# Two blocks with expert layers on one core: where the background work stands in the queues of VectorE and GpSimd

## Chip, cores and metric

The kernel runs on 1 core of one Trainium2 chip. The metric is the device time of one execution in microseconds (us), the median over several runs.

## What is computed

256 tokens (batch 1) of width 2048 pass through two blocks, all in fp32. A block is a mixer and then an expert layer, each added to its input:

```python
x = x + mixer(rmsnorm(x, g_mix))        # first block: latent attention and sparse attention, gated
x = x + peer_ffn(rmsnorm(x, g_ffn), w_q, sub_keys, u_emb, v_emb)
x = rmsnorm(x, g_final)                 # second block: the same with mLSTM and an S5 recurrence as mixer
```

The expert layer chooses, per token and for each of 8 heads, 16 of 16,384 experts, and the recurrence's matrices come from a few parameters:

```python
def peer_ffn(x):                          # 128 tokens at a time
    q = einsum('td,dhk->thk', x, w_q)     # 8 heads, each in two halves of 64
    s = einsum('thpc,hpnc->thpn', q, sub_keys)
    s1, i1 = top_k(s[:, :, 0], 16);  s2, i2 = top_k(s[:, :, 1], 16)
    top_s, pos = top_k(s1[..., :, None] + s2[..., None, :], 16)
    expert = (i1 * 128 + i2) at pos;  g = softmax(top_s)
    a = gelu(einsum('thkd,td->thk', u_emb[expert], x))
    return einsum('thk,thkd->td', g * a, v_emb[expert])

def s5(u):                                # 64 states for each of 64 groups
    dt = exp(log_dt);  a = exp(lam * dt)              # complex
    b = ((a - 1) / lam) * B
    state = scan(state * a + b @ u);  y = Re(C @ state) + d * u
```

## The kernel before

**Products.** All matrix products run over all experts: no weight is gathered. An fp32 operand is split in a high part and the rest (`w_hi` and `w_lo`, `hT_hi` and `hT_lo`), and each product is three matmuls, hi by hi, hi by lo, lo by hi, in `products` (L214; the matmul is L220). `weights_now` (L196) brings one weight tile of 128 x 2048 in two halves: DMAs on SyncE (L203), the cast to `w_hi` on ScalarE (L205), and the subtraction that makes `w_lo` on VectorE (L211) or, for the last `pool` columns, on GpSimd (L209). `w_raw`, `w_hi` and `w_lo` have four half buffers each, so two tiles can be in the making or in use.

**The expert layer** is `peer` (L328), called twice. After the query products and the top-k of the keys, two rounds `r` follow; each takes 64 of the 128 first keys:

- product U: 64 weight tiles, two for one `ps_u`; `hT` is the operand of all. For the first 28 tiles of round 0 GpSimd makes 768 of 2048 columns of `w_lo` (`UP`, `UN`).
- beside it the gates, a dense matrix of each token's weight for each expert: 32 groups of 8 tokens. `prepare` (L487) makes one-hot matrices of the chosen indices, `oh1` on GpSimd (L491; 6 of 8 tokens in round 0, `G0`, all in round 1, the rest on VectorE), then `oh2`, `rh` and `rl` on VectorE (L494, L498, L499). `use` multiplies them on TensorE into `ps_g` (L505, L506).
- product V: 64 weight tiles, with the coefficients (`coef_hi`, `coef_lo`, L259, L260) as the other operand. Its stationary operand starts on a multiple of 64 bytes of a partition.

In round 0 the gates need `routing` (L406) for the two blocks of 128 tokens: a top-k over candidates on VectorE and a choice by one-hot (`oh`, the multiply L462 on GpSimd, 128 x 2048).

**Background work.** Gates, routing and other side work are generators in the list `K.bg`. After each weight tile the foreground calls `K.step(n)` (L151), which runs their next pieces until a credit of `n` us is used up. A scheduler then sorts each engine's instructions, by its own model of the times, so what was emitted first need not stand first. `behind(ins)` (L188) adds a condition of order: what is emitted inside it stands on `ins`'s engine after `ins`. Before, background pieces have none.

**The preparation of the recurrence** is one such piece, `_s5_prepare` (L1094), for the second mixer; nothing needs it before. It is handed to the first expert layer as `later` and begins when the 32 groups of gates of round 0 are emitted, within product U (`st["groups"] == T // TG`, L539). It makes on VectorE long chains of small operations on `s_prm` (L1066 to L1163) and `s_work`; 16 tables of three operations on GpSimd (L1194, L1195, L1196), which go out by DMA (L1201, L1202 for the decay, copied on VectorE before); and eight times an expansion of 2 x 6 operations (L1212 to L1221), one on VectorE and one on GpSimd, with transposes and small products on TensorE between them. The first expansion reuses the tables' buffer.

**Addresses.** `hT` (L284) is two tiles of 16,384 bytes a partition in a pool at the top, above 448 bytes of padding (`pad3`). They start at 196,128 and 212,512 of a partition, 32 bytes past a multiple of 64. The same tiles hold the operands of the two output projections (`mh`, `ml` in `mix1`, `ch`, `cl` in `mix2`). `o_hi` and `o_lo` of the first mixer start on multiples of 64 (124,928 for the first).

**Names of stretches.** Cut where the first weight DMA of each product is issued: U1a 664 to 1152 us, V1a 1152 to 1528, U1b 1528 to 1904, V1b 1904 to 2252 in the first expert layer (a is round 0, b round 1); U2a 2790 to 3197, V2a to 3546, U2b to 3922, V2b to the end in the second.

Of the kernel before, what the change touches and what calls it, by code (L numbers as in the profile page):

```python
# [9 lines left out]
OP = mybir.AluOpType  # L10
AX = mybir.AxisListType

P = 128
T = 256
TB = 2
D = 2048
KD = D // P
# [16 lines left out]
class Ctx:  # L34


    def __init__(self, ctx, tc):
        self.tc, self.nc = tc, tc.nc
        nc = self.nc
# [4 lines left out]
        self.wp = pool("weights", 2)  # L44
        self.pad = pool("pad", 1)
        self.two = pool("pairs", 2)
        self.pad3 = pool("pad3", 1, side="right")
        self.top = pool("hT", 1, side="right")
        for p, n in ((self.pad, 0), (self.pad3, 448)):
            if n:  # L50
                nc.gpsimd.memset(p.tile([P, n // 4], F32, name="pad"), 0.0)
        self.ps = pool("psum", 2, space=bass.MemoryType.PSUM)
# [18 lines left out]
        self.fine = 0  # L71
        self.last = None

    def defer(self, fn):
# [76 lines left out]
    def step(self, n):  # L151


        self.credit = min(self.credit, 0.0) + n
        idle = 0
        while self.credit > 0 and idle < len(self.bg):
            lane = self.bg.pop(0)
            try:
                took = next(lane)
            except StopIteration:  # L160
                continue
            self.bg.append(lane)
            self.credit -= took
            idle = 0 if took else idle + 1

    def lane(self):
# [29 lines left out]
    def weights_now(self, src, n, pool):  # L196
        nc = self.nc
        self.fine -= 1
        h = n // 2
        raw, hi, lo = ([self.wp.tile([P, D // 2], d, name=nm, bufs=4)[:, :h] for _ in range(2)]  # L200
                       for nm, d in (("w_raw", F32), ("w_hi", F32R), ("w_lo", F32R)))
        for i in range(2):
            nc.sync.dma_start(raw[i], src[:, i * h:(i + 1) * h])  # L203
        for i in range(2):
            nc.scalar.copy(hi[i], raw[i])  # L205
        for i in range(2):
            m = max(0, min(h, (2 - i) * h - pool))
            if m < h:
                nc.gpsimd.tensor_tensor(lo[i][:, m:], raw[i][:, m:], hi[i][:, m:].bitcast(F32), op=OP.subtract)  # L209
            if m:  # L210
                nc.vector.tensor_tensor(lo[i][:, :m], raw[i][:, :m], hi[i][:, :m].bitcast(F32), op=OP.subtract)  # L211
        return Halves(hi, h), Halves(lo, h)
# [70 lines left out]

    def hT(self):  # L284
        return (self.top.tile([P, KD, T], F32R, name="hT_hi"),
                self.top.tile([P, KD, T], F32R, name="hT_lo"))

# [40 lines left out]
def peer(K, wq, keys, u, v, g_out, g_next=None, dst=None, later=None):  # L328
# [156 lines left out]
    def gates(r, on_pool):  # L485

        def prepare(t0):  # L487
            oh1 = K.two.tile([P, TG, P], F16, name="oh1", tag="two_a", bufs=2)
            for t in range(TG):
                e = nc.gpsimd if t < on_pool else nc.vector  # L490
                e.tensor_scalar(oh1[:, t], K.iota, i1T[:, t0 + t:t0 + t + 1], None, op0=OP.is_equal)  # L491
            oh2 = rp.tile([P, TG, NJ], F16, name="oh2", bufs=2)
# [42 lines left out]
    for r in range(2):  # L535
        st.update(done=0, groups=0, A=[rp.tile([P, 16, T], F32, name="acts", tag="acts", bufs=4) for _ in range(4)])
        K.bg.append(gates(r, 8 if r else G0))
        for jp in range(NJ // 2):
            if r == 0 and st["groups"] == T // TG and later is not None:  # L539
                K.bg.append(later(rp))  # L540
                later = None
            ps = K.ps.tile([P, 2, T], F32, name="ps_u", bufs=2)
# [17 lines left out]
        if later is not None:  # L560
            K.bg.append(later(rp))
            later = None
# [120 lines left out]
def mix1(K, I):  # L683
# [7 lines left out]
    ps_v = lambda shape: K.ps.tile(shape, F32, name="ps_v", bufs=4)  # L691

    grow = b8([P, D], "gain_row")[0:1]
    nc.sync.dma_start(grow, I["norm_mix_row"])
# [300 lines left out]
    for i in range(KD):  # L995
# [9 lines left out]
        nc.vector.tensor_tensor(m, m, g1, op=OP.add)  # L1005
    mh, ml = K.hT()
    for q in range(4):
# [268 lines left out]
def mix2(K, I, dram):  # L1276
# [332 lines left out]
    for h in range(MH):  # L1609
# [4 lines left out]
        ready["h"] = h + 1  # L1614
    ch, cl = K.hT()

# [180 lines left out]
```

## Time and profile before

| | |
|---|---|
| median of 3 runs | 4299.8 us (4299.35 to 4306.35) |
| the profiled execution, time | 4299.48 us |
| its span on the core | 4297.4 us |
| mean granted clock of TensorE | 0.981 |
| PE, DVE, ACT, POOL busy | 97%, 66%, 47%, 36% |

PE is TensorE's matmuls, PEld its weight loads, DVE VectorE, ACT ScalarE, POOL GpSimd, SP SyncE. A table by stretches has in each row the stretch in us and its length, then for each engine its busy time and, behind an x, its instructions, then the granted clock of TensorE (1.00 is 2.4 GHz, 0.50 is 1.2 GHz), the DMA engines' busy share and GB/s. A row of waits names the engine, tile and line that waited, what it waited for, and then us in total, times, and the longest in us. A group of instructions has line, engine, operation, out<-in with shapes, the count, and then busy us and the mean of one in ns. A timeline row has start and length in us, the instruction, how many in a row, and in brackets the idle time before it and what ended that.

### The profile page before, as it was taken

Reading aid. Unit: us, or ns where it says so; the run is one execution under the profiler, and the core shown is the slowest. Engines: PE = TensorE matmul, PEld = TensorE weight load, DVE = VectorE, ACT = ScalarE, POOL = GpSimd, SP = SyncE. Lnnn points to the kernel's source line nnn. Section 1 sums busy time; section 2 is a strip of 40 time slices with the busy share of each in tenths; the row PEclk is TensorE's granted clock in tenths of the full one; section 3 lists DMA queues with packets and bytes.
Section 4 is the critical chain, followed back from the end, with each engine's and each line's share of the span. In section 5 each row is a group of like instructions: output and inputs, shape, how many; then the busy total and the mean of one; then the engine's idle time right before and its main releaser. Section 6 shows DMA issues by size and latency. Waiting matters only on the chain. (4 is left out here: it accounts for less than half of the span.)

```text
span 4297.4 us, 74404 instructions
## 1 busy us (share of the span) xinstructions
PE 4149.5 (97%) x29233; PEld 3827.3 (89%) x29233; DVE 2831.5 (66%) x4666; ACT 2019.8 (47%) x2848; POOL 1535.1 (36%) x1318
## 2 busy tenths in 40 slices
PE   8999999888999999999998999999999999999999
PEld 7999989778888899998888998999998889999887
DVE  6775559887557656665556556798855556665565
ACT  5565443433344444445553455444445554444554
POOL 1100023789214147730005452369910006772000
PEclk9999999999999999999998999999999999999999
DMA  5445554454456655555666555545555555555555
GB/s 178 162 150 189 182 175 141 145 169 144 154 201 218 208 184 180 178 181 193 201 207 207 177 164 176 165 143 177 171 179 192 195 195 181 180 180 185 192 204 167
DMA packets 234160, 769.95 MB, mean 179 GB/s; under 512 B 44304, under 2 KB 46352, under 8 KB 233041
## 3 DMA queue, kind: packets, MB, share of 16 engines
q1 hardware_dynamic: 227906, 742.96, 52.5%
q0 software_dynamic: 5904, 22.25, 1.4%
q8 instruction: 229, 3.75, 0.3%
q14 instruction: 121, 0.99, 0.1%
HBM read 748.85 MB, written 16.25 MB: 178 GB/s over the span
## 5 line engine op out<-in xcount | busy, mean ns | idle before, releaser
L211 DVE TENSOR_TENSOR w_lo<-w_raw,w_hi 128x1024 fp32r<-128x1024 f32 (+3 forms) x1347 | 1631.8, 1244 | 1220.9 <-issue 941.6
L205 ACT CAST w_hi<-w_raw 128x1024 fp32r<-128x1024 f32 (+1 forms) x1388 | 1445.5, 1045 | 1603.9 <-PE ps_v L220 632.7
L220 PE MATMUL ps_u<-hT_hi,w_hi 128*128 128x256 f32 x5712 | 1404.0, 287 | 15.4 <-ACT acts L555 7.1
L220 PE MATMUL ps_u<-hT_lo,w_hi 128*128 128x256 f32 x5712 | 1387.1, 284 | 0.0
L491 POOL TENSOR_SCALAR oh<-iota_h,i1T 128x128 f16<-128x128 f16 x896 | 910.1, 1033 | 659.8 <-PE ps_v L220 492.7
L220 PEld LDWEIGHTS ps_u<-hT_hi,w_hi 128*128 128x128 f32 x5712 | 1098.6, 192 | 18.2 <-ACT acts L555 7.6
L220 PEld LDWEIGHTS ps_u<-hT_lo,w_hi 128*128 128x128 f32 x5712 | 1098.8, 192 | 1.9
L220 PE MATMUL ps_u<-hT_hi,w_lo 128*128 128x256 f32 x5712 | 739.2, 281 | 32.0 <-POOL w_lo L209 21.2
L220 PEld LDWEIGHTS ps_u<-hT_hi,w_lo 128*128 128x128 f32 x5712 | 699.8, 189 | 36.2 <-POOL w_lo L209 22.2
L220 PE MATMUL ps_v<-w_hi,coef_lo 128*128 128x512 f32 x2048 | 692.8, 390 | 2.4 <-DVE coef_lo L260 2.3
L220 PE MATMUL ps_v<-w_hi,coef_hi 128*128 128x512 f32 x2048 | 689.5, 390 | 0.0
L220 PE MATMUL ps_v<-w_lo,coef_hi 128*128 128x512 f32 x2048 | 512.5, 389 | 0.0
L220 PEld LDWEIGHTS ps_v<-w_hi,coef_lo 128*128 128x128 f32 x2048 | 383.1, 188 | 83.2 <-DVE coef_lo L260 4.4
L220 PEld LDWEIGHTS ps_v<-w_hi,coef_hi 128*128 128x128 f32 x2048 | 384.5, 188 | 79.7
L220 PEld LDWEIGHTS ps_v<-w_lo,coef_hi 128*128 128x128 f32 x2048 | 384.3, 188 | 79.6
L209 POOL TENSOR_TENSOR w_lo<-w_raw,w_hi 128x768 fp32r<-128x768 f32 (+3 forms) x159 | 310.1, 1957 | 353.3 <-PE ps_u L220 154.5
L259 ACT CAST coef_hi<-acts 128x512 fp32r<-128x512 f32 x256 | 159.4, 624 | 181.1 <-PE ps_v L220 177.8
L260 DVE TENSOR_TENSOR coef_lo<-acts,coef_hi 128x512 fp32r<-128x512 f32 x256 | 184.3, 721 | 6.0 <-ACT coef_hi L259 6.0
L119 POOL TENSOR_TENSOR normed<-x,gain 128x512 f32<-128x512 f32 x22 | 37.1, 1708 | 367.5 <-DVE x L96 280.1
L505 PE MATMUL ps_g<-rh,oh 128*128 128x64 f16 x1024 | 85.5, 197 | 40.8 <-POOL oh L491 35.5
L498 DVE TENSOR_TENSOR rh<-oh,g_hi 128x512 f16<-128x512 f16 x128 | 102.4, 800 | 19.8 <-PE ps_g L506 19.8
L515 ACT ACTIVATE acts<-ps_g 128x128 f32<-128x128 f32 (+7 forms) x318 | 60.6, 255 | 113.9 <-DVE acts L512 113.7
(490 smaller groups left out, 3573.2 us busy)
## 6 DMA issues: line engine op xcount, KB each, us to landing
w_raw<-in_p_u SPq DMA_DIRECT2D x512, 512.0 KB, 4.1
w_raw<-in_p_v SPq DMA_DIRECT2D x512, 512.0 KB, 4.3
w_raw<-in_in_gates SPq DMA_DIRECT2D x64, 512.0 KB, 4.0
w_raw<-in_w_out SPq DMA_DIRECT2D x64, 512.0 KB, 3.8
w_raw<-in_p_q SPq DMA_DIRECT2D x48, 512.0 KB, 4.1
w_raw<-in_in_t SPq DMA_DIRECT2D x38, 512.0 KB, 4.1
w_raw<-in_w_ab SPq DMA_DIRECT2D x32, 512.0 KB, 4.0
w_raw<-in_in_qk SPq DMA_DIRECT2D x32, 512.0 KB, 3.7
```

Of the source, the lines that this page charges most:

```text
L119: eng.tensor_tensor(self.normed_cols(tb, c), self.x[:, tb, cc], gb[:, cc], op=OP.mult)
L205: nc.scalar.copy(hi[i], raw[i])
L209: nc.gpsimd.tensor_tensor(lo[i][:, m:], raw[i][:, m:], hi[i][:, m:].bitcast(F32), op=OP.subtract)
L211: nc.vector.tensor_tensor(lo[i][:, :m], raw[i][:, :m], hi[i][:, :m].bitcast(F32), op=OP.subtract)
L220: self.last_mm = self.nc.tensor.matmul(out, lhsT=a, rhs=b, start=start, stop=stop)
L259: self.nc.scalar.copy(hi, src)
L260: return self.nc.vector.tensor_tensor(lo, src, hi.bitcast(F32), op=OP.subtract)
L491: e.tensor_scalar(oh1[:, t], K.iota, i1T[:, t0 + t:t0 + t + 1], None, op0=OP.is_equal)
L498: nc.vector.tensor_tensor(rh, oh2, b2(gh), op=OP.mult)
L505: nc.tensor.matmul(ps[:, t], lhsT=oh1[:, t], rhs=rh[:, t], start=True, stop=False)
L515: nc.scalar.activation(dst(nd, 16), src(nd, 16), AF.Copy, scale=1.0 / GS)
```

## The change

It keeps in `K.lo` the `w_lo` subtraction that was emitted last on VectorE and on GpSimd, and on GpSimd the last one-hot too. `step` runs each piece of background inside `behind` of both, so a piece can no longer stand on these two engines ahead of them. `later` is no longer started within product U, but after it, wrapped in `pin`, which puts the same condition on each of its pieces wherever they are run from. `hT` becomes one tile with 32 spare bytes: with the standard shift it starts where it did; with shift 0, for the operands of the two output projections, it starts at 196,096 and 212,480. The first mixer makes an 8-column tile first, so that its other tiles lie 32 bytes further up (`o_hi` at 124,960).

```diff
@@ Ctx.__init__ @@
-        self.pad = pool("pad", 1)
...
-        for p, n in ((self.pad, 0), (self.pad3, 448)):
-            if n:
-                nc.gpsimd.memset(p.tile([P, n // 4], F32, name="pad"), 0.0)
+        nc.gpsimd.memset(self.pad3.tile([P, 112], F32, name="pad"), 0.0)
...
+        self.lo = [None, None]
@@ step @@
-                took = next(lane)
+                with self.behind(self.lo[0]), self.behind(self.lo[1]):
+                    took = next(lane)
...
+    def pin(self, lane):
+
+        while True:
+            with self.behind(self.lo[0]), self.behind(self.lo[1]):
+                took = next(lane, None)
+            if took is None:
+                return
+            yield took
@@ weights_now @@
-                nc.gpsimd.tensor_tensor(lo[i][:, m:], raw[i][:, m:], hi[i][:, m:].bitcast(F32), op=OP.subtract)
+                self.lo[1] = nc.gpsimd.tensor_tensor(lo[i][:, m:], raw[i][:, m:], hi[i][:, m:].bitcast(F32), op=OP.subtract)
             if m:
-                nc.vector.tensor_tensor(lo[i][:, :m], raw[i][:, :m], hi[i][:, :m].bitcast(F32), op=OP.subtract)
+                self.lo[0] = nc.vector.tensor_tensor(lo[i][:, :m], raw[i][:, :m], hi[i][:, :m].bitcast(F32), op=OP.subtract)
@@ hT @@
-        return (self.top.tile([P, KD, T], F32R, name="hT_hi"),
-                self.top.tile([P, KD, T], F32R, name="hT_lo"))
+    def hT(self, shift=8):
+
+        both = self.top.tile([P, 2 * KD * T + 8], F32R, name="hT")[:, shift:shift + 2 * KD * T]
+        both = both.rearrange("p (two k t) -> p two k t", two=2, k=KD)
+        return both[:, 0], both[:, 1]
@@ prepare, in peer @@
-                e.tensor_scalar(oh1[:, t], K.iota, i1T[:, t0 + t:t0 + t + 1], None, op0=OP.is_equal)
+                one = e.tensor_scalar(oh1[:, t], K.iota, i1T[:, t0 + t:t0 + t + 1], None, op0=OP.is_equal)
+                if t < on_pool:
+                    K.lo[1] = one
@@ product U, in peer @@
-            if r == 0 and st["groups"] == T // TG and later is not None:
-                K.bg.append(later(rp))
-                later = None
...
         if later is not None:
-            K.bg.append(later(rp))
+            K.bg.append(K.pin(later(rp)))
             later = None
@@ mix1 @@
+    nc.gpsimd.memset(wt([P, 8], "pad", 1), 0.0)
...
-    mh, ml = K.hT()
+    mh, ml = K.hT(0)
@@ mix2 @@
-    ch, cl = K.hT()
+    ch, cl = K.hT(0)
```

Lines move by 8 to 11: the subtractions are L217 and L219 in the changed kernel, the routing's multiply L472, the one-hots L501, the tables L1204 to L1206, the chains on `s_prm` L1076 and on.

**POOL, where the routing and the first groups of gates stand in U1a.** A row is line, operation, out<-in and shape, and xN where N alike follow each other; `oh` is the routing's product, `oh_8483` the one-hot `oh1` of a group (its buffer's number), `s_bc` a load for the preparation. Before:

```order
L209 TENSOR_TENSOR w_lo<-w_raw,w_hi 128x768 x13
L462 TENSOR_TENSOR oh<-oh,idx 128x2048
L209 TENSOR_TENSOR w_lo<-w_raw,w_hi 128x768
L462 TENSOR_TENSOR oh<-oh,idx 128x2048
L209 TENSOR_TENSOR w_lo<-w_raw,w_hi 128x768
L1230 DMA s_bc<-in_s_bc 128x512
L209 TENSOR_TENSOR w_lo<-w_raw,w_hi 128x768 x4
L491 TENSOR_SCALAR oh_8483<-iota_h,i1T 128x128 x6
L491 TENSOR_SCALAR oh_8567<-iota_h,i1T 128x128 x6
L209 TENSOR_TENSOR w_lo<-w_raw,w_hi 128x768 x2
L462 TENSOR_TENSOR oh<-oh,idx 128x2048 x2
L209 TENSOR_TENSOR w_lo<-w_raw,w_hi 128x768
```

Now:

```order
L217 TENSOR_TENSOR w_lo<-w_raw,w_hi 128x768 x15
L472 TENSOR_TENSOR oh<-oh,idx 128x2048 x2
L217 TENSOR_TENSOR w_lo<-w_raw,w_hi 128x768 x4
L501 TENSOR_SCALAR oh_8479<-iota_h,i1T 128x128 x6
L501 TENSOR_SCALAR oh_8563<-iota_h,i1T 128x128 x6
L217 TENSOR_TENSOR w_lo<-w_raw,w_hi 128x768 x3
L501 TENSOR_SCALAR oh_8673<-iota_h,i1T 128x128 x6
L217 TENSOR_TENSOR w_lo<-w_raw,w_hi 128x768
```

The routing's multiplies stand two in a row behind 15 subtractions, where single subtractions stood between them; the second pair, which stood before the third group of one-hots, comes later. Twelve one-hots stand in a row in both, and three subtractions between them and the next group.

**POOL, the second half of U1a.** The one-hots of four groups and what stands between them. Before:

```order
L491 TENSOR_SCALAR oh_9888<-iota_h,i1T 128x128 x6
L1213 TENSOR_TENSOR s_prm<-s_bc,s_prm 128x512
L1194 TENSOR_TENSOR s_work<-s_work 128x256 x2
L1195 TENSOR_TENSOR s_prm<-s_work 128x256
L1194 TENSOR_TENSOR s_work<-s_work 128x256 x2
L491 TENSOR_SCALAR oh_9989<-iota_h,i1T 128x128 x6
L1196 TENSOR_TENSOR s_work<-s_work,s_prm 128x256
L491 TENSOR_SCALAR oh_10086<-iota_h,i1T 128x128 x6
L1195 TENSOR_TENSOR s_prm<-s_work 128x256
L1196 TENSOR_TENSOR s_work<-s_work,s_prm 128x256
```

Now, the last groups of one-hots of U1a and the first operations of the preparation:

```order
L501 TENSOR_SCALAR oh_11985<-iota_h,i1T 128x128 x6
L501 TENSOR_SCALAR oh_12086<-iota_h,i1T 128x128 x6
L501 TENSOR_SCALAR oh_12183<-iota_h,i1T 128x128 x6
L1110 DMA s_prm<-in_s_lam 128x96
L1240 DMA s_bc<-in_s_bc 128x512 x2
L1212 DMA s_tab<-s_decay 128x256 x2
L1223 TENSOR_TENSOR s_prm<-s_bc,s_prm 128x512
L1204 TENSOR_TENSOR s_work<-s_work 128x256 x2
L1205 TENSOR_TENSOR s_prm<-s_work 128x256
```

The tables (`s_work`, `s_prm`) have left the place between the one-hots; all of them stand behind the last one.

**DVE, where the preparation begins.** `s_prm` are its parameters, `acts` the coefficients, `rh` and `rl` the gates' operands. Before, within U1a:

```order
L211 TENSOR_TENSOR w_lo<-w_raw,w_hi 128x1024
L1076 SCALAR_TENSOR_TENSOR s_prm<-s_prm 128x32
L211 TENSOR_TENSOR w_lo<-w_raw,w_hi 128x256
L498 TENSOR_TENSOR rh<-oh_9031,g_hi 128x512
L512 SCALAR_TENSOR_TENSOR acts<-ps_g,acts 128x16x8
L491 TENSOR_SCALAR oh_9022<-iota_h,i1T 128x128 x2
L499 TENSOR_TENSOR rl<-oh_9031,g_lo 128x512
L1077 SCALAR_TENSOR_TENSOR s_prm<-s_prm 128x32
L494 TENSOR_TENSOR oh_9330<-iota_h,i2T 128x512
L1111 TENSOR_TENSOR s_prm<-s_prm 128x32
L1114 TENSOR_TENSOR s_prm<-s_prm 128x32
L1066 TENSOR_SCALAR s_prm<-s_prm 128x32
```

Now, about the first `coef_lo` of V1a (the preparation's first row stands 28 rows ahead of it):

```order
L219 TENSOR_TENSOR w_lo<-w_raw,w_hi 128x1024
L1124 TENSOR_TENSOR s_prm<-s_prm 128x32
L1086 SCALAR_TENSOR_TENSOR s_prm<-s_prm 128x32
L268 TENSOR_TENSOR coef_lo<-acts,coef_hi 128x512
L1086 SCALAR_TENSOR_TENSOR s_prm<-s_prm 128x32 x2
L1087 SCALAR_TENSOR_TENSOR s_prm<-s_prm 128x32
L684 TENSOR_SCALAR s_prm<-s_prm 128x32
L685 TENSOR_SCALAR s_prm<-s_prm 128x32
L687 SCALAR_TENSOR_TENSOR s_prm<-s_prm 128x32 x3
L219 TENSOR_TENSOR w_lo<-w_raw,w_hi 128x1024
L687 SCALAR_TENSOR_TENSOR s_prm<-s_prm 128x32
L219 TENSOR_TENSOR w_lo<-w_raw,w_hi 128x1024
```

The chains on `s_prm` stood between subtractions and gates of U1a, and now stand between subtractions and `coef_lo` of V1a.

## Rows read from the trace of the kernel before

**Rows 1.** The page: busy time of each engine, and PE in the forty slices.

```profile
PE 4149.5 (97%) x29233; PEld 3827.3 (89%) x29233; DVE 2831.5 (66%) x4666; ACT 2019.8 (47%) x2848; POOL 1535.1 (36%) x1318
...
PE   8999999888999999999998999999999999999999
```

**Rows 2.** Table by stretches: U1a, V1a, U1b, V1b and U2a, every engine.

```profile
664.00:1152.00 488.00, 418.23 (x3613) 406.22 (x3612) 403.04 (x993) 180.49 (x284) 342.25 (x308) 0.92 0.45 149
1152.00:1528.00 376.00, 373.62 (x1807) 312.40 (x1805) 241.40 (x245) 182.07 (x207) 76.03 (x70) 1.00 0.62 206
1528.00:1904.00 376.00, 376.00 (x3516) 372.00 (x3515) 239.25 (x328) 167.53 (x272) 257.14 (x256) 1.00 0.54 180
1904.00:2252.00 348.00, 348.00 (x1604) 291.03 (x1604) 197.69 (x194) 178.14 (x206) 16.09 (x10) 1.00 0.60 200
...
2790.00:3197.00 407.00, 389.94 (x3601) 386.80 (x3600) 333.33 (x649) 175.52 (x279) 287.66 (x226) 0.97 0.51 166
```

**Rows 3.** What PE waited for in U1a up to 890 us.

```profile
PE ps_u L220 <- POOL w_lo L209: 13.3, 3, 10.4
PE ps_u L220 <- DVE w_lo L211: 6.4, 8, 3.4
```

**Rows 4.** What PE waited for in U1a from 890 us on.

```profile
PE ps_g L505 <- POOL oh L491: 33.7, 36, 5.9
```

**Rows 5.** What PE waited for in U2a.

```profile
PE ps_u L220 <- POOL w_lo L209: 7.9, 2, 5.8
PE ps_u L220 <- DVE w_lo L211: 4.2, 3, 2.4
...
PE ps_g L505 <- POOL oh L491: 1.8, 2, 1.3
```

**Rows 6.** The table by stretches, tile s_prm alone: DVE, ACT, POOL; U1a and V1a.

```profile
664.00:1152.00 488.00, 59.83 (x216) 0.55 (x2) 47.15 (x45) 0.92 0.45 149
1152.00:1528.00 376.00, 34.20 (x41) 0.00 (x0) 57.36 (x36) 1.00 0.62 206
```

**Rows 7.** The table by stretches, tile s_work alone, all engines; U1a.

```profile
664.00:1152.00 488.00, 0.00 (x0) 0.00 (x0) 9.54 (x30) 0.00 (x0) 62.38 (x66) 0.92 0.45 149
```

**Rows 8.** Timeline of POOL in U1a, from 764 and from 911 us.

```profile
764.19 19.10 POOL L491 TENSOR_SCALAR oh<-iota_h,i1T 128x128 f16<-128x128 f16 x12
...
911.80 7.05 POOL L491 TENSOR_SCALAR oh<-iota_h,i1T 128x128 f16<-128x128 f16 x6
918.82 1.52 POOL L1196 TENSOR_TENSOR s_work<-s_work,s_prm 128x256 f32<-128x256 f32 x1
920.32 7.29 POOL L491 TENSOR_SCALAR oh<-iota_h,i1T 128x128 f16<-128x128 f16 x6
```

**Rows 9.** Groups of instructions on POOL in U1a.

```profile
L491 POOL TENSOR_SCALAR oh<-iota_h,i1T 128x128 f16<-128x128 f16 x192 | 191.4, 1012 | 1.9 <-PE ps_g L506 1.7
...
L462 POOL TENSOR_TENSOR oh<-oh,idx 128x2048 f32<-128x2048 f32 x4 | 19.4, 4867 | 7.1 <-DVE oh L459 7.1
L1196 POOL TENSOR_TENSOR s_work<-s_work,s_prm 128x256 f32<-128x256 f32 x16 | 17.7, 1104 | 0.6
```

**Rows 10.** Groups of instructions on DVE in V1a, each shape apart.

```profile
L211 DVE TENSOR_TENSOR w_lo<-w_raw,w_hi 128x1024 fp32r<-128x1024 f32 x130 | 164.6, 1301 | 131.2 <-issue 118.9 <-ACT w_hi L205 12.2
```

**Rows 11.** Groups of instructions on DVE in V1b, each shape apart.

```profile
L211 DVE TENSOR_TENSOR w_lo<-w_raw,w_hi 128x1024 fp32r<-128x1024 f32 x128 | 156.7, 1263 | 148.7 <-issue 144.9 <-ACT w_hi L205 3.7
L260 DVE TENSOR_TENSOR coef_lo<-acts,coef_hi 128x512 fp32r<-128x512 f32 x60 | 42.9, 715 | 0.2 <-ACT coef_hi L259 0.2
```

**Rows 12.** Table of four 50 us stretches with one kind of product each.

```profile
400.00:450.00 50.00, 50.00 (x423) 50.00 (x422) 25.74 (x31) 19.55 (x22) 0.00 (x0) 1.00 0.55 188
550.00:600.00 50.00, 50.00 (x216) 40.24 (x215) 25.31 (x24) 21.89 (x29) 7.75 (x5) 1.00 0.55 186
1950.00:2000.00 50.00, 50.00 (x223) 41.40 (x222) 26.67 (x27) 25.10 (x28) 0.00 (x0) 1.00 0.59 198
3150.00:3200.00 50.00, 50.00 (x431) 50.00 (x430) 23.63 (x22) 21.15 (x22) 0.00 (x0) 1.00 0.58 187
```

More of the change, by code (lines that the diff above doesn't have):

```diff
@@ L282, in rsqrt @@
         return r
-    def hT(self):
-        return (self.top.tile([P, KD, T], F32R, name="hT_hi"),
-                self.top.tile([P, KD, T], F32R, name="hT_lo"))
+    def hT(self, shift=8):
+        both = self.top.tile([P, 2 * KD * T + 8], F32R, name="hT")[:, shift:shift + 2 * KD * T]
+        both = both.rearrange("p (two k t) -> p two k t", two=2, k=KD)
+        return both[:, 0], both[:, 1]
     def norm_T(self):
```

## The prediction

> **What bounds the kernel now.** I read the page first: PE is busy for 97% of the span, DVE for 66%, POOL for 36%, and the row of the forty slices (107 us each) shows PE below 9 tenths in the first slice, in 8 to 10 and in 22 alone [rows 1]. So only places where PE waits can give time back. The table by stretches shows which [rows 2]. U1b and U2a are the measures for U1a: all three multiply 64 weight tiles and make 32 groups of gates. U1b takes 376 us with PE busy for all of it; U2a, which has routing as well, 407; U1a 488. U1a so loses 112 us against U1b: PE is idle for 488 - 418.2 = 69.8, and the granted clock of 0.92, a mean over 2.4 GHz and stretches at 1.2 GHz, costs about 0.08 x 488 = 39. U2a loses 31, of which 407 - 389.9 = 17.1 is idle time. A microsecond of idle time has thus cost 112 / 69.8 = 1.6 us in U1a and 1.8 in U2a.
>
> The waits of PE say for whom: in U1a up to 890 us 13.3 us for w_lo from POOL and 6.4 for w_lo from DVE [rows 3], after it 33.7 in 36 waits for POOL's one-hots [rows 4]; in U2a 7.9 and 4.2 for w_lo and only 1.8 for one-hots [rows 5]. What U1a has and U2a has not is the preparation of the recurrence: it keeps DVE busy for 59.8 us there (tile s_prm) and POOL for 62.4 (tile s_work) [rows 6, 7]. The timeline of POOL shows how it hurts: about 919 us a table operation stands between two blocks of six one-hots, for which PE waits [rows 8].
>
> **The change part by part.**
>
> (a) *U1a loses the preparation.* By the order rows its table operations leave POOL's queue between the one-hots, and they stand behind the last one. DVE falls to 403.0 - 59.8 = 343 us and POOL to 342.3 - 62.4 = 280, beside 333.3 and 287.7 in U2a [rows 2]. The floor is U1b's 376. What stays late is seen in the order too: POOL still has twelve one-hots in a row before the next w_lo, and two multiplies of the routing in a row. The twelve take 19.1 us now [rows 8], and behind them PE has its longest wait for w_lo, 10.4 us [rows 3]; at 1.012 us each [rows 9] they take 12.1, and that wait falls by some 5 to about 6. I leave 4 us for the two multiplies (2 x 4.9 us [rows 9] in front of a w_lo that is two tiles ahead, at 376 / 64 = 5.9 us a tile) and 3 for the first and the last group of gates. 13 us of idle time at U2a's 1.8 is 24: U1a takes 400, a gain of **88**. Bounds: 48, at 440 (U2a's 31 lost us; 18 for the 10 us of work that DVE has more than there, at 1.8; 9 for the long wait, if it stays whole; and 6, one more wait as long as PE's longest for a one-hot, 5.9 us), and 104, at 384 (8 lost us).
>
> (b) *The weights' parts go first.* Routing on DVE and POOL can no longer stand ahead of a w_lo that was emitted before it. In U2a this is aimed at 7.9 + 4.2 us of waits [rows 5]. The order moves the second routing there by some seven tiles, but leaves the first where it was; half of the 12.1 us at 1.8 is **10**. Bounds: 22 (all of them) and -10 (routing that is late by one block of six one-hots, 6 us at 1.6). In U1b and U2b the queues alternate weights and gates as before, and in U1b PE is busy throughout [rows 2]: nothing.
>
> (c) *V1a takes the preparation.* PE's share of it, transposes and small products, is in V1a already, by the order. DVE goes from 241.4 to 301 of 376 us, POOL from 76 to 138 [rows 2]. But it comes early: by the order, nearly all of the DVE part but eight table copies and one expansion stands within the first 15 weight tiles, some 52 of the 59.8 us (a copy is 9.54 / 30 = 0.3 us [rows 7]; V1a has 41 operations on s_prm now, seven expansions, at 34.2 / 7 = 4.9 us [rows 6]). A tile of V takes 348 / 64 = 5.4 us of PE [rows 2] and 2 x 1.263 + 0.715 = 3.2 us of DVE [rows 11]. So DVE needs 15 x 3.2 + 52 = 100 us where PE needs 82; two tiles of weights in advance cover 11 of the 18. The other 7 are the price, **+7**. Bounds: 0 (some small operations stand in idle moments) and 27, if the lead is no cover, 18 x 1.5. POOL's 16 tables are three operations each, of which the longest takes 1.104 us [rows 9], at most 53 us; they lie beside PE work. The first expansion waits for the last of them, which falls near tile 25, before the first transposes.
>
> (d) *Addresses.* Before, hT starts at byte 196,128 of a partition, 32 bytes past a multiple of 64; the operands of both output projections now start at 196,096, and the first mixer's tiles move by 32 bytes. The rows with one kind of product each: V, whose stationary operand starts on a multiple of 64, makes 223 matmuls in 50 us, the output projection 216, so 224.2 against 231.5 ns; products with hT as moving operand alone make 431, those shared with o_hi and o_lo (on a multiple of 64) 423 [rows 12], so 116.0 against 118.2, and if the second half alone is slow, 120.4. Two projections of 384 matmuls at 7.3 ns are 5.6 us, 768 matmuls on o at 4.4 ns 3.4 us: **-9**. Bounds: 0, if the address is not the cause, and -11.
>
> The few small memsets and the first mixer's angles, which now stand behind w_lo, change waits of 3 us at most; PE has no such row in rows 3 to 5, and I cost them at nothing.
>
> **Sum.** The profiled execution took 4299.5 us, 2.1 more than its span and 0.3 less than the median. 4299.5 - 88 - 10 + 7 - 9 = 4199.5; I predict **4199 us**.
>
> **Rivals.** What can be told from no change here is 0.2%, 8.6 us.
>
> *Half of it (0.21).* Routing, not the preparation, keeps U1a long: 440 (a gain of 48), nothing in (b), +10 in (c), -4 in (d): 4258. For it: PE waits 10.4 us before 890, where POOL has no table operation yet [rows 3]. Against it: all of the 33.7 us of one-hot waits come after 890 [rows 4], and U2a has 1.8.
>
> *A port lock in V1a (0.08).* The w_lo of V takes 1.301 us where POOL works beside it and 1.263 where POOL has 16 us of work [rows 2, 10, 11]; 130 of them make 5 us for 76 us of POOL. That is a small price, and another 62 us of POOL would add 4. But the table work comes in one piece, beside DVE's own 52 us. If each of its 53 us stopped DVE for as long, DVE would need 25 x 3.2 + 52 + 53 = 185 us in 25 tiles where PE needs 136; less 11 of lead, 38 lost, 38 x 1.6 = 61 in place of 7: 4253; with half of (b) and (d) gone too, 4263. The Trainium skill, SBUF — State Buffer, section Who interferes with whom, states that a VectorE instruction with two SBUF inputs and a GpSimd instruction that reads SBUF take one shared port, and that the loser is stopped for the whole instruction. By that rule it is this rival; of that, the mean of w_lo above bears out less than a tenth (5 of 76 us).
>
> *The pin turns round (0.06).* Background behind a w_lo that waits for a buffer which PE has yet to free starts later; PE then meets gates whose one-hots are not made, in all four U products. If each of 128 groups waited the 33.7 / 36 = 0.94 us of U1a now [rows 4], at 1.6, 192 us would be lost where 112 + 31 are lost now: +49, and 4299.5 + 49 + 7 - 9 = 4346, slower. It decides from 0.75 us a group: (112 + 31 + 2 + 8.6) / (128 x 1.6). Against it: by the order, one-hots and weights alternate in U1b as before, and POOL, which has no w_lo there, works 257 of 376 us.
>
> *It doesn't do what it says (0.05).* The extra edges leave PE's order as it was; if waits for other work of the same queues took the place of each, the time would stay within 8.6 us of 4300.
>
> *All of it (0.04).* U1a and U2a both come to 384: -104 - 23 - 9 = 4163.
>
> **How the numbers follow.** The forecast, 4199, has the rest, 0.56. The first two rivals and the last are faster as well: 0.56 + 0.21 + 0.08 + 0.04 = 0.89; same 0.05; slower 0.06. The forecast's own bounds, -104 - 22 + 0 - 11 and -48 + 10 + 27 + 0, are 4162 and 4288, and hardly all fall on one side; 4165 to 4272 holds nearly all of the forecast and of the half, leaving out the two cases of no gain and the ends.
>
> **What would show it.** U1a at 385 to 415 us with PE's one-hot waits under 10 us, and no s_prm or s_work on DVE or POOL before its end; U2a at 385 to 407; V1a within 370 to 390 with PE at 0.98 or more; 222 matmuls in 50 us of the output projection and 428 in the stretch with o_hi. A V1a over 400 would make (c) wrong, a U1a over 425 (a), and new waits of PE in U1b (b).

## The result and the profile after

The changed kernel takes 4229.6 us (median of 4 runs, 4226.2 to 4233.1) against 4299.6 (4298.1 to 4306.4): a ratio of 0.9834, 95% interval 0.9817 to 0.9851. It is 70 us faster; 100 us (4199) were forecast, within 4165 to 4272. Its profiled execution took 4231.5 us, with a span of 4229.7. All ratios here compare fast runs alone: one of twelve executions of e3_addresses_only took 5782 us, at a granted clock of 0.65, and is left out of its ratio.

The page of the changed kernel, as [rows 1]:

```profile
PE 4116.1 (97%) x29233; PEld 3804.3 (90%) x29233; DVE 2818.4 (67%) x4666; ACT 2018.1 (48%) x2846; POOL 1564.2 (37%) x1319
...
PE   8999999999989999999999999999999999999998
```

PE fell below 9 tenths in three of the forty slices, 1, 12 and the last, where it had been five. Slices 8 to 10 and 22 are at 9 tenths or more now; slice 12 is new and lies in V1a.

The table by stretches, as [rows 2]: U1a, V1a, U1b, V1b and U2a, cut at the first weight DMA of each product (then PE, PEld, DVE, ACT, POOL busy, the granted clock, the DMA share and GB/s):

```profile
657.70:1061.10 403.40, 388.94 (x3616) 384.34 (x3615) 336.50 (x759) 175.44 (x278) 289.07 (x228) 0.98 0.51 169
1061.10:1466.30 405.20, 379.47 (x1799) 316.02 (x1798) 293.91 (x470) 182.66 (x209) 154.04 (x149) 0.97 0.60 200
1466.30:1842.80 376.50, 376.50 (x3518) 372.33 (x3517) 243.94 (x336) 169.56 (x274) 259.01 (x257) 1.00 0.55 181
1842.80:2191.50 348.70, 348.70 (x1609) 291.56 (x1608) 197.72 (x195) 178.46 (x207) 16.07 (x10) 1.00 0.60 199
2726.70:3129.50 402.80, 386.21 (x3606) 383.37 (x3605) 323.47 (x642) 175.31 (x279) 289.22 (x226) 0.98 0.51 168
```

The cuts of both kernels give the terms of the sum, in us of each one's profiled execution:

| stretch | before | after | difference | forecast |
|---|---|---|---|---|
| up to U1a | 664.3 | 657.7 | -6.6 | (d), -9 with the row of the second mixer |
| U1a | 488.3 | 403.4 | -84.9 | (a), -88 |
| V1a | 375.2 | 405.2 | +30.0 | (c), +7 |
| U1b and V1b | 724.7 | 725.2 | +0.5 | 0 |
| second mixer and queries | 537.3 | 535.2 | -2.1 | in (d) |
| U2a | 407.6 | 402.8 | -4.8 | (b), -10 |
| the rest | 1100.0 | 1100.2 | +0.2 | 0 |
| span | 4297.4 | 4229.7 | -67.7 | -100 |

One term left its bounds, V1a's: +30.0 where (c) had 0 to 27. The waits of PE in the changed kernel (us in total, times, longest), in U1a, as [rows 3, 4]:

```profile
PE ps_u L228 <- POOL w_lo L217: 9.1, 5, 2.8
PE ps_u L228 <- DVE w_lo L219: 2.7, 2, 1.6
PE ps_g L517 <- POOL oh L501: 1.9, 3, 1.2
```

in U2a, as [rows 5]:

```profile
PE ps_u L228 <- POOL w_lo L217: 12.0, 5, 5.2
PE ps_u L228 <- DVE w_lo L219: 2.9, 2, 2.1
PE ps_g L517 <- POOL oh L501: 1.7, 1, 1.7
```

and in V1a for `coef_lo`, before (the only waits of PE there) and after:

```profile
PE ps_v L220 <- DVE coef_lo L260: 2.3, 3, 1.0
```

```profile
PE ps_v L228 <- DVE coef_lo L268: 21.1, 6, 10.6
```

The 33.7 us of waits for one-hots in U1a have come down to 1.9. In V1a the waits for `coef_lo` have gone from 2.3 to 21.1 us. The same stretch in pieces says when they come:

```profile
1061.00:1101.00 40.00, 40.00 (x247) 35.96 (x246) 28.66 (x77) 20.00 (x23) 0.00 (x0) 1.00 0.57 186
1101.00:1141.00 40.00, 40.00 (x178) 33.10 (x178) 34.77 (x123) 20.20 (x22) 0.00 (x0) 1.00 0.60 197
1141.00:1181.00 40.00, 40.00 (x178) 33.14 (x177) 35.51 (x81) 20.21 (x22) 23.43 (x23) 1.00 0.65 213
1181.00:1221.00 40.00, 33.85 (x149) 27.37 (x147) 25.14 (x24) 17.04 (x19) 32.26 (x37) 1.00 0.63 205
1221.00:1261.00 40.00, 33.43 (x149) 27.74 (x150) 27.86 (x23) 14.71 (x17) 30.19 (x29) 0.87 0.59 196
```

For 120 us PE loses nothing, though 206 of the 257 operations on `s_prm` that DVE does in V1a fall there (DVE is busy for up to 35.5 us of 40). The loss begins after 1181, where DVE is *less* busy, 25.1 us. So DVE didn't lack time; it stood still. What it waited for in V1a:

```profile
DVE s_work L1222 <- DMA s_w<-s_work: 20.6, 4, 6.9
...
DVE s_work L1226 <- POOL s_prm L1205: 12.1, 1, 12.1
```

And its timeline about the longest wait:

```profile
1208.35 0.69 DVE L1222 TENSOR_TENSOR s_work<-s_bc,s_prm 128x512 f32<-128x512 f32 x1 [0.52 <-POOL s_prm L1205]
1208.96 0.68 DVE L268 TENSOR_TENSOR coef_lo<-acts,coef_hi 128x512 fp32r<-128x512 f32 x1
1209.77 3.00 DVE L219 TENSOR_TENSOR w_lo<-w_raw,w_hi 128x1024 fp32r<-128x1024 f32 x2
1224.92 0.69 DVE L1226 TENSOR_TENSOR s_work<-s_bc,s_prm 128x512 f32<-128x512 f32 x1 [12.14 <-POOL s_prm L1205]
...
1226.83 0.68 DVE L268 TENSOR_TENSOR coef_lo<-acts,coef_hi 128x512 fp32r<-128x512 f32 x1
```

The first expansion has begun at 1208.35 and goes on at 1224.92, when POOL's last tables (L1205) have read the buffer that it overwrites. `coef_lo` of the next weight tile stands behind it in DVE's queue. That needs nothing of POOL, and ACT's part of it was done by 1216.7, as this row of ACT's timeline shows (start, length):

```profile
1216.06 0.62 ACT L267 CAST coef_hi<-acts 128x512 fp32r<-128x512 f32 x1 [0.76 <-PE ps_v L228]
```

PE waits 10.6 us for it, and the clock of the stretch from 1221 to 1261 is 0.87 (table above):

```profile
1227.57 2.08 PE L228 MATMUL ps_v<-w_hi,coef_lo 128*128 128x512 f32 x4 [10.64 <-DVE coef_lo L268]
```

The Trainium skill, PSUM — Partial Sum Buffer, section Engine vs sequencer instructions, states that the queues of ScalarE, VectorE and GpSimd are strict first in, first out; the trace agrees, with these 12.14 us in which `coef_lo` doesn't overtake.

### The profile page after: what moved, and what is told of

It is laid out like the page before. It is cut to its first block, busy times and chain, and to the rows that moved or that the text cites. A ratio compares the mean times of both kernels' runs of the same rounds, so it can differ in the third digit from the quotient of the medians.

```text
span 4229.7 us, 74587 instructions
## 1 busy us (share of the span) xinstructions
PE 4116.1 (97%) x29233; PEld 3804.3 (90%) x29233; DVE 2818.4 (67%) x4666; ACT 2018.1 (48%) x2846; POOL 1564.2 (37%) x1319
## 5 line engine op out<-in xcount | busy, mean ns | idle before, releaser
L219 DVE TENSOR_TENSOR w_lo<-w_raw,w_hi 128x1024 fp32r<-128x1024 f32 (+3 forms) x1347 | 1635.1, 1247 | 1179.6 <-issue 887.1
L228 PE MATMUL ps_u<-hT,w_hi 128*128 128x256 f32 x11424 | 1435.1, 282 | 1.9 <-DVE gate L1462 1.9
L228 PEld LDWEIGHTS ps_u<-hT,w_hi 128*128 128x128 f32 x11424 | 1377.2, 189 | 4.9 <-DVE gate L1462 2.2
L501 POOL TENSOR_SCALAR oh<-iota_h,i1T 128x128 f16<-128x128 f16 x896 | 928.7, 1054 | 603.3 <-PE ps_v L228 432.1
L228 PE MATMUL ps_u<-hT,w_lo 128*128 128x256 f32 x5712 | 735.9, 281 | 26.7 <-POOL w_lo L217 21.1
L228 PEld LDWEIGHTS ps_u<-hT,w_lo 128*128 128x128 f32 x5712 | 697.6, 189 | 29.7 <-POOL w_lo L217 23.1
L228 PE MATMUL ps_v<-w_hi,coef_lo 128*128 128x512 f32 x2048 | 695.7, 392 | 23.2 <-DVE coef_lo L268 21.1
L217 POOL TENSOR_TENSOR w_lo<-w_raw,w_hi 128x768 fp32r<-128x768 f32 (+3 forms) x159 | 313.1, 1978 | 340.8 <-PE ps_u L228 133.8
L228 PE MATMUL ps_v<-w_hi,hT 128*128 128x512 f32 (+2 forms) x576 | 125.4, 367 | 1.5 <-ACT hT L267 1.1
L228 PEld LDWEIGHTS ps_v<-w_hi,hT 128*128 128x128 f32 x576 | 100.0, 188 | 20.0 <-ACT hT L267 1.3
L506 DVE TENSOR_TENSOR oh<-iota_h,i2T 128x512 f16<-128x512 f16 x128 | 97.9, 764 | 0.3
```

What stands on the lines that cost most here:

```text
L217: self.lo[1] = nc.gpsimd.tensor_tensor(lo[i][:, m:], raw[i][:, m:], hi[i][:, m:].bitcast(F32), op=OP.subtract)
L219: self.lo[0] = nc.vector.tensor_tensor(lo[i][:, :m], raw[i][:, :m], hi[i][:, :m].bitcast(F32), op=OP.subtract)
L228: self.last_mm = self.nc.tensor.matmul(out, lhsT=a, rhs=b, start=start, stop=stop)
L501: one = e.tensor_scalar(oh1[:, t], K.iota, i1T[:, t0 + t:t0 + t + 1], None, op0=OP.is_equal)
L506: nc.vector.tensor_tensor(oh2, K.iota[:, None, r * NJ:(r + 1) * NJ].to_broadcast([P, TG, NJ]), b2(i2T), op=OP.is_equal)
```

## The experiments

The stretches of every run, in us of one profiled execution each, cut as above; then the median of the times, and the ratio to the kernel before, run beside it, with its 95% interval:

| run | U1a | V1a | U2a | time | ratio |
|---|---|---|---|---|---|
| before | 488.3 | 375.2 | 407.6 | 4299.6 | |
| after | 403.4 | 405.2 | 402.8 | 4229.6 | 0.9834 (0.9817 to 0.9851) |
| e1_place_only | 489.5 | 374.7 | 407.5 | 4296.5 | 0.9998 (0.9988 to 1.0007) |
| e2_edges_only | 404.8 | 404.5 | 403.1 | 4233.7 | 0.9848 (0.9833 to 0.9862) |
| e3_addresses_only | 491.9 | 375.5 | 408.3 | 4291.9 | 0.9988 (0.9979 to 0.9997) |
| e4_w1_on_act | 402.5 | 393.3 | 403.4 | 4219.3 | 0.9817 (0.9802 to 0.9831) |
| e5_expand_later | 403.4 | 379.8 | 404.6 | 4210.1 | 0.9803 (0.9786 to 0.9819) |
| e6_both | 403.3 | 385.1 | 404.5 | 4211.8 | 0.9808 (0.9791 to 0.9824) |
| e7_pin_preparation | 417.4 | 403.4 | 405.6 | 4254.9 | 0.9905 (0.9888 to 0.9921) |
| e8_dve_edge_only | 407.0 | 400.6 | 403.9 | 4232.6 | 0.9855 (0.9839 to 0.9872) |
| e9_first_groups_dve | 400.4 | 386.7 | 400.2 | 4206.6 | 0.9792 (0.9775 to 0.9808) |
| e10_fewer_tables | 404.3 | 377.6 | 403.9 | 4201.2 | 0.9779 (0.9763 to 0.9796) |
| e11_routing_on_dve | 398.7 | 383.8 | 393.6 | 4196.6 | 0.9763 (0.9747 to 0.9780) |

**Which part of the change gained.** e1 to e3 each put one part on the kernel before.

e1_place_only:

```diff
-            if r == 0 and st["groups"] == T // TG and later is not None:
-                K.bg.append(later(rp))
-                later = None
             ps = K.ps.tile([P, 2, T], F32, name="ps_u", bufs=2)
```

> The kernel before with one part of the change: the preparation begins after the first round's product U, with nothing put behind the weights' parts and the old addresses. Theory P (the place of the preparation brought U1a's 85 us): U1a 400 to 412 us against 488 before and 403 after, V1a 400 to 410 as after, U2a 407 as before; time 4299.5 - 82 + 30 = 4248 (4238 to 4258). Theory Q (the order edges brought it): U1a 440 us or more, time 4270 or more.

Measured: 4296.5 us, no difference. Theory P fell. The table by stretches of e1, for tile `s_prm` alone (DVE, ACT, POOL), says why:

```profile
800.00:900.00 100.00, 52.57 (x203) 0.55 (x2) 0.60 (x1) 0.97 0.47 158
```

DVE does 52.6 us of the preparation between 800 and 900 us, in the middle of U1a, though the code begins it after U1a. Where a piece is emitted doesn't say where it stands: the scheduler moved it up.

e2_edges_only:

```diff
-                took = next(lane)
+                with self.behind(self.lo[0]), self.behind(self.lo[1]):
+                    took = next(lane)
...
+                self.lo[1] = nc.gpsimd.tensor_tensor(lo[i][:, m:], raw[i][:, m:], hi[i][:, m:].bitcast(F32), op=OP.subtract)
...
+                self.lo[0] = nc.vector.tensor_tensor(lo[i][:, :m], raw[i][:, :m], hi[i][:, :m].bitcast(F32), op=OP.subtract)
...
+                if t < on_pool:
+                    K.lo[1] = one
```

> The kernel before with the other part: all background is put behind the weights' parts and one-hots already emitted, the preparation still begins within U1a, old addresses. Theory P: U1a 465 to 490 us, V1a 376, U2a 403; time 4290 (4272 to 4300). Theory Q: U1a 425 us or less, time 4240 or less.

Measured: U1a 404.8, V1a 404.5, time 4233.7: the whole change but for the addresses, and theory Q. The conditions of order hold the preparation back, and they also bring V1a its loss. The wrapper `pin` and the later start aren't needed for either: e2 has neither.

e3_addresses_only has `hT(self, shift=8)`, `hT(0)` for both output projections, and the 8-column tile of `mix1`.

> The kernel before with the addresses of the change alone (output projections' operands on a multiple of 64 bytes, first mixer's tiles 32 bytes up). Theory A (the address sets the rate): 6.6 us less ahead of U1a and 2 less in the second mixer, time 4291 (4289 to 4293), over 221 matmuls in 50 us of the output projection against 216. Theory B (the address is not the cause, the 8.7 us came with the new order): 4299 to 4300, 216 matmuls.

Measured: ratio 0.9988, at most 0.9997, so faster, by 5 us (1 to 9). Its table by stretches of 50 us, in the stretch with `o_hi` and in the output projection, as [rows 12]:

```profile
394.00:444.00 50.00, 50.00 (x431) 50.00 (x430) 25.93 (x33) 20.49 (x22) 0.00 (x0) 1.00 0.54 188
545.00:595.00 50.00, 50.00 (x222) 41.42 (x221) 26.16 (x25) 21.95 (x27) 7.53 (x5) 1.00 0.55 190
```

431 and 222 matmuls where it was 423 and 216, theory A. The way up to U1a is 5.4 us shorter, the second mixer with its queries 5.0 (532.3); U1a itself came out 3.6 longer in this execution. In all traces together, the way up to U1a takes 663 to 665 us with the old addresses (before, e1, e2, e7) and 658 to 661 with the new ones. For the second mixer the two groups overlap, 534 to 537 and 530 to 535, so that share isn't clear of the spread.

**What in U1a was the preparation, what the routing.** e7_pin_preparation is the kernel before with the later start of e1 and with `pin`, which alone sets conditions:

```diff
                 took = next(lane)
...
-            K.bg.append(later(rp))
+            K.bg.append(K.pin(later(rp)))
```

> The kernel before with the preparation alone begun after product U and put behind the weights' parts; routing and gates stand where they stood before, old addresses. Theory R (two causes in U1a: the preparation made the 33.7 + 5.3 us of waits after 890 us, routing the 30 us before): U1a 418 to 434 us, U2a 407 as before, V1a about 405; time 4267 (4256 to 4276). Theory S (the preparation alone kept U1a long): U1a 412 or less, time 4250 or less.

Measured: U1a 417.4, time 4254.9, both a little under R's ranges and over S's. What PE waited for there:

```profile
PE ps_u L230 <- POOL w_lo L219: 12.5, 3, 10.3
PE ps_u L230 <- DVE w_lo L221: 6.5, 4, 4.5
PE ps_g L517 <- POOL oh L501: 2.6, 4, 1.3
```

The one-hots' waits are gone and the others are as in [rows 3]: two causes, as R has it. Holding back the preparation gave 488.3 - 417.4 = 71 us of U1a's 85, the routing and the gates behind the weights' parts the other 14. The twelve one-hots in front of the long wait, in e7 and in the changed kernel:

```profile
765.79 19.10 POOL L501 TENSOR_SCALAR oh<-iota_h,i1T 128x128 f16<-128x128 f16 x12
```

```profile
752.06 12.03 POOL L501 TENSOR_SCALAR oh<-iota_h,i1T 128x128 f16<-128x128 f16 x12
```

With the preparation gone they still take 19.10 us, as before [rows 8], and PE's wait behind them is still 10.3; both fall only when the rest of the background is held back too (12.03 and 2.8).

e8_dve_edge_only is the changed kernel with `with self.behind(self.lo[0]):` alone in both places.

> The changed kernel without the conditions on POOL: background is put behind the weights' parts on DVE alone. The routing's multiplies move one or two subtractions on POOL, the preparation stays out of U1a. If DVE's edge does the work: U1a 400 to 408 us, U2a 400 to 408, time 4230 (4222 to 4238). If POOL's edges carry a part: U1a over 412, time over 4240.

Measured: U1a 407.0, U2a 403.9, time 4232.6, so DVE's edge does the work. POOL's tables wait for DVE's chains anyway: in the changed kernel POOL stands for 134.8 us, up to 1152 us, until DVE has made `s_prm`.

**Where V1a's 30 us came from.** e4_w1_on_act:

```diff
-        g.dma_start(dram["w1"][i], W[:, 0])
+        nc.scalar.dma_start(dram["w1"][i], W[:, 0])
```

> The changed kernel with one DMA issue moved: an expansion's result w1 is sent out from ACT's queue, behind the copies that complete it, in place of POOL's, where it stands behind other work. Theory H (V1a lost its 30 us because DVE's queue stands still behind expansions that wait for w1's buffer or for POOL's tables): DVE's waits for this DMA fall from 20.6 to under 6 us, PE's waits of 2.1, 1.0, 3.4, 2.3 and 3.4 us from 1266 us on go, the first wait of 10.6 stays; V1a 386 to 394 us against 405, time 4216 (4210 to 4221). Theory L (DVE and POOL slow each other down at a shared port, so DVE lacks time): V1a 402 to 408, time 4226 to 4233.

Measured: V1a 393.3, time 4219.3, theory H. (The interval of its ratio overlaps the changed kernel's; the verdict rests on V1a and the waits.) DVE's waits in its V1a:

```profile
DVE s_work L1226 <- POOL s_prm L1205: 10.7, 1, 10.7
...
DVE s_work L1222 <- DMA s_w<-s_work: 5.5, 4, 2.6
```

The waits for the DMA fell from 20.6 to 5.5 us and the first wait stayed, with 9.7 us of PE.

e5_expand_later:

```diff
+    yield 9
     ahead = inputs(0)
     yield 1.5
```

> The changed kernel with the first expansion of the preparation emitted some four weight tiles (22 us) later in V1a, so that POOL's tables can be done when DVE reaches it; the table work and the copies stay where they were, beside the subtractions. Theory H (DVE stands still behind an expansion that waits for POOL): the wait of 12.1 us of DVE and PE's wait of 10.6 us go, the waits for w1's DMA stay; V1a 385 to 393 us against 405, time 4214 (4208 to 4220). Theory L (DVE and POOL slow each other at a shared port and DVE lacks time): V1a 402 to 408, time 4226 to 4233.

Measured: V1a 379.8, time 4210.1. In these two traces that is 25 of the 30 us, more than H gave it. The size is less sure than the sign: the three other runs that have this edit and all tables (e6, e9, e11) come to 383.8 to 386.7, and those without either edit (after, e2, e7, e8) to 400.6 to 405.2; the ratios' intervals of e5 and of the changed kernel overlap by a hair. One of the eight expansions now stands in U1b, which takes 377.1 us against 376.5. In e5's V1a DVE waits for no table, PE has 7.0 us of waits for `coef_lo` against 21.1, and DVE's subtraction is slower than ever:

```profile
PE ps_v L228 <- DVE coef_lo L268: 7.0, 5, 2.6
```

```profile
DVE s_work L1222 <- DMA s_w<-s_work: 4.2, 2, 3.4
```

```profile
L219 DVE TENSOR_TENSOR w_lo<-w_raw,w_hi 128x1024 fp32r<-128x1024 f32 x130 | 180.9, 1421 | 70.0 <-issue 51.2 <-ACT w_hi L213 10.1 <-PE ps_v L228 8.0
```

The waits for w1's DMA fell to 4.2 us by themselves, so they too seem to follow from the first stop; how, isn't shown. Theory L is out as the cause of most of the loss: the tables stand where they did, a subtraction takes 1.421 us against 1.383, and most of the time is back.

e6_both has both edits.

> The changed kernel with both edits, the first expansion later and w1's DMA issued from ACT. Theory H: V1a comes to 375 to 384 us (376 before), time 4203 (4198 to 4210). Theory L: over 390.

Measured: V1a 385.1, time 4211.8, H's ranges just missed. The two edits don't add up: they remove the same waits, by e4 and e5, and e5 alone took 4210.1.

e10_fewer_tables is e5 (its one-hots stand on POOL as there), and makes the first 4 of the 16 tables only, so that its output lacks the rest:

```diff
+            if i > 1:
+                continue
             g.tensor_tensor(tab[:, part], big(part), fine(0), op=OP.mult)
```

> As the run above, with 12 of the 16 tables of the recurrence left out on POOL (36 operations, some 40 us), so its output lacks them. It measures what POOL's table work itself costs V1a. Theory H (nothing but the order costs there): V1a 376 to 380 us against 380, the mean of w_lo falls from 1.42 towards 1.30 us without any gain of time. Theory L (a shared port takes DVE's time): V1a 372 or less, or the time at least 8 us under that of the run above.

Measured: V1a 377.6 against e5's 379.8, w_lo 1.379 us against 1.421, time 4201.2 against 4210.1. V1a speaks for H; the time, 8.9 us less, meets the second sign of L. Neither is clear: V1a differs by 7 us among the runs with e5's edit and all tables (379.8 to 386.7), and the intervals of the two ratios overlap. POOL works 34 us less in V1a here (147.6 to 113.4 us); whether that is worth nothing or up to 9 us is left open.

**What is left in U1a and U2a.** e9_first_groups_dve, on e5:

```diff
-                e = nc.gpsimd if t < on_pool else nc.vector
+                e = nc.gpsimd if t < on_pool and (r or t0 >= 2 * TG) else nc.vector
```

> The changed kernel with the first expansion later (as in the run before) and the one-hots of the first two groups of round 0 made on DVE in place of POOL, so that POOL has no twelve one-hots in a row before the next subtraction. Theory T (what is left of U1a's and U2a's loss against 376 us comes from subtractions on POOL that stand behind them): PE's longest waits for POOL's w_lo, 2.8 us in U1a and 5.2 in U2a, go; U1a 394 to 399 us against 403, U2a 392 to 398 against 404, time 4195 (4188 to 4202) against 4210. Theory D (DVE has no room in this stretch): new waits for DVE's w_lo take their place, time 4207 to 4215.

Measured: U1a 400.4, U2a 400.2, time 4206.6: the stretches lie between the two theories, the time at the edge of D's range. PE's waits in its U2a:

```profile
PE ps_u L228 <- POOL w_lo L217: 5.9, 3, 3.3
PE ps_u L228 <- DVE w_lo L219: 4.9, 3, 2.2
...
PE ps_g L517 <- ACT acts L527: 1.7, 1, 1.7
```

The waits for POOL's w_lo halved, 12.0 to 5.9 us, and DVE's w_lo and ACT took 3.7 us back.

e11_routing_on_dve, on e9:

```diff
-            nc.gpsimd.tensor_tensor(oh, oh, i4[:, :, half, None, :].to_broadcast([P, NH, SEL, SEL]), op=OP.mult)
+            nc.vector.tensor_tensor(oh, oh, i4[:, :, half, None, :].to_broadcast([P, NH, SEL, SEL]), op=OP.mult)
```

> As the run with the first groups' one-hots on DVE, and the routing's four multiplies of 128 x 2048 on DVE as well (2.3 us each there by the nearest operation of that shape, 4.9 on POOL). Theory T: the waits for POOL's w_lo behind them (some 1 to 3 us each) go too: U1a 388 to 396, U2a 386 to 394, time 4185 (4175 to 4195). Theory D: DVE's waits grow by as much, time as in the run before or longer.

Measured: U2a 393.6, U1a 398.7, time 4196.6, U1a and the time just above T's ranges; the multiply took 3.54 us on DVE, not 2.3. The waits that T named didn't go. PE's for POOL's w_lo in U2a are now one:

```profile
PE ps_u L228 <- POOL w_lo L217: 8.9, 1, 8.9
```

Of U2a's 6.6 us against e9 only 2.6 are idle time of PE; where the rest comes from isn't shown. It is the lowest time here: 33 us under the changed kernel's median, and 2.4% under the kernel before.

## Why the prediction was right, and where not

*The direction and U1a.* (a) gave 88 us and 84.9 came: the one-hots' waits went from 33.7 to 1.9 us, PE's idle time is 403.4 - 388.9 = 14.5 us where 13 were left for it, and the loss against U1b is 27 us, at 1.9 for each idle one. Another 15.6 us of PE's waits before, for `acts` (6.4 and 5.3) and `w_hi` (3.9) from ACT, which the prediction doesn't name, went as well. That it came so close is in part luck. (a) counted under the preparation what e7 sets apart: 71 us for the preparation, 14 for the routing and the gates in front of the weights' parts. The fall of the twelve one-hots from 19.1 to 12.1 us and of the wait behind them was one of (a)'s steps; it came (12.03 us, and a wait of 2.8 and not 6), but not from the preparation (e7: 19.10 and 10.3).

*What does it.* That the table operations would leave U1a was read from the order of the whole change, and so the sum was right whichever part caused it. The later place in the code is not the cause (e1), the edges are (e2), and DVE's alone suffice (e8).

*V1a: the step that failed.* (c) said "the other 7 are the price", with bounds of 0 to 27, and +30.0 came. Its argument was DVE's load in the first 15 tiles, 100 us of work against 82 of PE. That part cost nothing: PE was busy for all of its first 120 us. (c) also said that the first expansion waits for POOL's last table "before the first transposes", and gave this no price. But the wait stops DVE's own queue, in which the next `coef_lo` stands. e5 shows it: with the expansion four tiles later, V1a is back within 5 us of what it took before (within 12 in e6, e9 and e11). The kernel before shows the same stop on DVE, unpriced, in U1a, where the first expansion stood then:

```profile
DVE s_work L1216 <- POOL s_prm L1195: 5.4, 1, 5.4
DVE s_work L1212 <- POOL s_prm L1195: 5.4, 1, 5.4
```

In the changed kernel the first expansion stands behind the 22nd `coef_lo` on DVE, and on POOL the tables that it waits for are 16 x 3 operations:

```profile
L1206 POOL TENSOR_TENSOR s_work<-s_work,s_prm 128x256 f32<-128x256 f32 x16 | 20.5, 1278 | 0.6
L1205 POOL TENSOR_TENSOR s_prm<-s_work 128x256 f32<-128x256 f32 x16 | 15.3, 954 | 0.6
...
L1204 POOL TENSOR_TENSOR s_work<-s_work 128x256 f32<-128x256 f32 x16 | 14.8, 944 | 6.5 <-DMA s_tab<-s_work 6.5
```

Their price was right, 50.6 us where (c) allowed 53. Their place was not: they begin 98 us into V1a, behind DVE's chains, and the last read that the expansion waits for ends 164 us into it, some 30 tiles of 5.4 us and not 25. The 0.3 us of a table copy in (c) was read from a row of `s_work` that holds no copies; a copy takes 0.28 us in the kernel before and 0.62 beside the tables, which changes little.

*The port.* The rival of a port lock in V1a gave 4253 to 4263 and isn't what happened, but its mechanism is there. The groups of DVE, first with POOL idle (1061 to 1141 us), then beside the tables (1141 to 1208), when POOL is busy for 46.2 us:

```profile
L219 DVE TENSOR_TENSOR w_lo<-w_raw,w_hi 128x1024 fp32r<-128x1024 f32 x30 | 36.2, 1222 | 16.8 <-issue 8.5 <-PE ps_v L228 7.7 <-PE ps_u L228 0.6
```

```profile
L219 DVE TENSOR_TENSOR w_lo<-w_raw,w_hi 128x1024 fp32r<-128x1024 f32 x24 | 36.1, 1533 | 5.1 <-issue 4.7 <-PE ps_v L228 0.4
```

The second stretch as a whole, every engine:

```profile
1141.00:1208.00 67.00, 64.92 (x287) 53.44 (x286) 56.35 (x100) 32.78 (x36) 46.16 (x48) 1.00 0.65 215
```

A subtraction takes 1.533 us against 1.222: 24 x 0.311 = 7.5 us for 46.2 of POOL, a sixth, in the subtractions alone (`coef_lo`, 0.798 us against 0.681, adds 11 x 0.117 = 1.3). POOL's side shows it too. The same table operation beside DVE's subtractions, and while DVE stands still:

```profile
1205.13 1.62 POOL L1206 TENSOR_TENSOR s_work<-s_work,s_prm 128x256 f32<-128x256 f32 x1
```

```profile
1220.67 0.73 POOL L1206 TENSOR_TENSOR s_work<-s_work,s_prm 128x256 f32<-128x256 f32 x1
```

The Trainium skill, SBUF — State Buffer, section Who interferes with whom, states that a VectorE instruction with two SBUF inputs contends with a GpSimd instruction that reads SBUF, for a port that is locked to one of them. The trace agrees that the two hinder each other; DVE lost far less by it than the rival supposed, which took it to be as much as POOL worked. DVE's spare time covered most of it (e5).

*U2a.* (b) gave 10 and 4.8 came, and not by its step. The subtractions' waits didn't halve, they grew: 12.0 + 2.9 us against 7.9 + 4.2. The twelve one-hots in a row stayed, with one wait of 5.2 us behind them. PE's idle time is as before, 16.6 us against 17.1; nearly all of the 4.8 us is busy time, at a clock of 0.98 against 0.97. The gain comes with the conditions of order (402.8 to 404.6 us in seven runs that have them, 405.6 to 408.3 in the four where routing and gates have none); how they make it is open.

*Addresses.* (d) gave 9, and 6.6 + 2.1 = 8.7 came; 222 and 431 matmuls where 222 and 428 were named, and e3 shows it apart, for the way up to U1a clear of the spread, for the second mixer not.

*The other rivals.* "The pin turns round" is out: U1b and U2b are as before within 0.5 us. Of "all of it", 384 us for U1a and for U2a, and of "half of it", 440 for U1a, neither came: U1a is 403 and U2a 403.

## What to carry to other kernels

Where a scheduler sorts the queues, the place of a call doesn't keep work out of a stretch; a condition of order on the engine that must not be overtaken does, and the order it writes has to be read. Background work on an in-order queue is cheap while it only uses time (120 us of V1a, at up to 89% of DVE, cost nothing) and dear while it waits: ask of each moved operation what it waits for, and what stands behind it. Where it waits for another engine, put work between them (four tiles here) before making either faster.

## What was not expected of the hardware

The two operands of a matmul want opposite starts here. As the stationary operand `hT` of the output projection gives 222 matmuls in 50 us on a multiple of 64 bytes and 216 when it starts 32 past one; as the moving operand of 256 columns `o_hi` and `o_lo`, which share their stretch with `hT`, give 431 when they start 32 past and 423 on a multiple (e3). DVE's subtraction of 128 x 1024 slowed from 1.222 to 1.533 us beside POOL's tables, and PE was still busy for 64.9 of those 67 us. A table operation on POOL took 0.73 us while DVE stood still and 1.62 beside its subtractions.
